# Both orders of a query block in one attention step

## The chip, the cores and the metric

The kernel runs on one core of one Trainium2 chip. The metric is device time in microseconds of one execution, as the median of several. A difference of about 0.2% (some 4.3 us) is the least that a measurement of this kernel can tell from none.

## The reference

Two layers of a hybrid decoder over 512 tokens of width 1024, all in 32-bit floats. Each layer projects x to queries, keys and values of a windowed attention, to those of a retention, and to gates; merges the two branches; then runs a SwiGLU feed-forward. Both sublayers end in a residual and a layer norm. What the change touches is the attention:

```python
for gi, (window, dilation) in enumerate(ATTN_GROUPS):      # (128,1), (512,4), (2048,16)
    o, lse = _dilated_window_attention(q_a[:, :, gi], k_a[:, :, gi], v_a[:, :, gi], ...)
...
s = jnp.einsum('bghnqe,bghnke->bghnqk', qs, kb).astype(jnp.float32) * (Dh ** -0.5)
s = s + bias[None, None, :, None]
m = jnp.max(s, axis=-1, keepdims=True)
p = jnp.exp(s - m)
l = jnp.sum(p, axis=-1, keepdims=True)
o = jnp.einsum('bghnqk,bghnke->bghnqe', (p / l).astype(v.dtype), vb)
...
wts = jax.nn.softmax(jnp.stack(lses, axis=0), axis=0)
y_a = jnp.sum(wts[..., None] * jnp.stack(outs, axis=0), axis=0)
```

There are three groups of six heads, each head 64 wide. A query attends to keys at distances that are multiples of its group's dilation, within the window. The three groups' outputs are mixed with weights that follow from their softmax denominators.

## The kernel before

TensorE (PE) runs nearly all the time on projections. A 32-bit operand is split into a high part (`whi`, `xh`; cast on ACT, line 353 or 94) and a low part (`wlo`, `xl`; subtracted on DVE, line 359 or 95), and a product is three matmuls, high by high, high by low and low by high (`mm3`). Most projections are done as seven products of halves instead of eight (`wide`, `tall`), whose operands are sums of blocks (`xs`; sums of `raw` tiles on DVE, line 375, or in the DMA). Their sums are in PSUM tiles named `ps`, and ACT and DVE copy them out and combine them (`sn`). Weight parts are in rings of four tiles each, raw weights in a ring of eight.

The attention runs beside the projections. Six heads are taken as three pairs (`hp`), and `attention_pair` makes for each pair a list of small operations. A list `side` holds them; each time a projection has emitted three matmuls, `tick` adds to a credit, and for each whole credit the next operation of the list is emitted. `pace(us)` sets the rate so that the list lasts about so long; an operation `nothing` only takes a place. `drain()` emits what is left. The framework's scheduler may then set an engine's instructions in another order than that of emission. Each engine runs its own in order.

A block is 128 queries of both heads of the pair, in one of two orders (`od`): in order 0 the tokens are in their own order, for the group of dilation 1, with 256 keys (128 for the first block); in order 1 they are gathered by their place modulo 4, and hold the groups of dilations 4 and 16, with 128 keys each. Four query blocks (`i`, NI = 4) by two orders are eight blocks a pair. A block goes through three steps:

- `scores(i, od)`: matmuls of 64 contraction rows (one head's width), one head on the upper and one on the lower half of the array, into two PSUM tiles `px` (one a head). DVE adds the bias and takes the maximum (line 571), ACT takes the exponential and its sum (line 573), into a tile `s` of a ring of six (`wk`, tag `w2`), which also holds `sn` and others.
- `turn(i, od)`: PE transposes the exponentials by 128 x 128 (line 582) into the first `px`, and ACT copies them to a tile `sT` of the same ring (line 583).
- `values(i, od)`: matmuls whose result is 64 partitions of a head, both heads side by side, into the second `px`; ACT copies them to `y` (line 595).

For the first two pairs the order at each place is `scores` of block t, `values` of block t-2, `turn` of block t-1; for the last pair it is `turn` of t-1, `scores` of t, `values` of t-1. After the last block `swap` sends maxima and sums of order 1 through DRAM, and a `tail` of operations, inserted into the next pair's list, weighs and adds the groups' outputs.

Of the kernel before, what the change touches and what calls it, by code (L numbers as in the profile page):

```python
# [11 lines left out]
F32 = mybir.dt.float32  # L12
F32R = mybir.dt.float32r
I32 = mybir.dt.int32
AF = mybir.ActivationFunctionType
ALU = mybir.AluOpType
# [3 lines left out]
P = 128  # L20
# [3 lines left out]
NI = S // P  # L24
DEPTH = 2
HD = 64
# [28 lines left out]
def hybrid_kernel(ctx, tc, x, rel_bias, w_in, b_in, w_attn_proj, w_ret_proj, w_out,  # L55
# [491 lines left out]
    def attention_pair(hp, qk, v, yp, bias, yaT):  # L547
# [7 lines left out]
        def scores(i, od):  # L555
            tk = slice(i * P, (i + 1) * P)
            pxs = [psum() for _ in range(2)]
            j0 = 1 if od == 0 and i == 0 else 0
            prs = [slice(hh * HD, (hh + 1) * HD) for hh in range(2)]
            if od == 0:  # L560
                for px, pr in zip(pxs, prs):
                    mm(px[:, j0 * P:2 * P], qk[0][pr, 0, tk], qk[0][pr, 1, (i - 1 + j0) * P:(i + 1) * P], True, True)
            else:
                for j in range(2):
                    for px, pr in zip(pxs, prs):
                        mm(px[:, j * P:(j + 1) * P], qk[1 + j][pr, 0, tk], qk[1 + j][pr, 1, tk], True, True)
            s = wk.tile([P, 2, 2 * P], F32, tag="w2", name="s")
            n0 = j0 * P
            for hh in range(2):
                m_, l_ = nm[:, od, i, hh:hh + 1], ls[:, od, i, hh:hh + 1]  # L570
                dve.tensor_tensor_reduce(out=s[:, hh, n0:], in0=pxs[hh][:, n0:2 * P], in1=bias[hp][hh][:, od, n0:],
                                         scale=-1.0, scalar=3e38, op0=ALU.add, op1=ALU.min, accum_out=m_)
                act.activation(out=s[:, hh, n0:], in_=s[:, hh, n0:], func=AF.Exp, bias=m_, scale=-1.0, accum_out=l_)
            wrk[i, od] = (pxs, s, j0)

        def turn(i, od):
            pxs, s, j0 = wrk[i, od]
            sT = wk.tile([P, 2, 2 * P], F32, tag="w2", name="sT")
            px = pxs[0].rearrange("p (h c) -> p h c", h=2)
            for hh in range(2):  # L580
                for j in range(j0, 2):
                    pe.transpose(px[:, hh, j * P:(j + 1) * P], s[:, hh, j * P:(j + 1) * P], ident)  # L582
            act.copy(out=sT[:, :, j0 * P:], in_=px[:, :, j0 * P:])
            latest["sT"] = sT
            wrk[i, od] = (pxs, sT, j0)

        def values(i, od):
            pxs, sT, j0 = wrk.pop((i, od))
            px = pxs[1]
            vs = (v[i - 1][:, 0] if i else None, v[i][:, 0]) if od == 0 else (v[i][:, 1], v[i][:, 2])  # L590
            for j in range(j0, 2):
                for hh in range(2):
                    cs = slice(hh * HD, (hh + 1) * HD)
                    mm(px[cs, :P], vs[j][:, cs], sT[:, hh, j * P:(j + 1) * P], j == j0, j == 1)
            act.copy(out=y[:, od, i], in_=px[:, :P])
# [61 lines left out]
        blocks = [(i, od) for i in range(NI) for od in range(2)]  # L657
        ops = []
        order = ((0, scores), (2, values), (1, turn)) if hp < 2 else ((1, turn), (0, scores), (1, values))
        for t in range(len(blocks) + 2):  # L660
            for lag, f in order:
                if 0 <= t - lag < len(blocks):
                    ops.append(lambda f=f, b=blocks[t - lag]: f(*b))
                elif t >= len(blocks):
                    ops.append(nothing)
            if t == 0:
                ops += [nothing] * 2
# [712 lines left out]
```

## Time and profile before

| what | value |
|---|---|
| median of the runs | 2147.03 us (2146.54 to 2148.25, 3 runs) |
| span of the profiled execution | 2144.4 us, first to last instruction; the page gives no other time of that execution |
| median less that span | 2.6 us |
| PE busy | 2129.8 us, 13914 matmul records |
| DVE busy | 1492.6 us |
| ACT busy | 1066.1 us |
| DMA | 351.32 MB, mean 164 GB/s |

In a profile's rows, PE is the matmul, PEld its weight load, DVE, ACT and POOL the other engines. A row names line, engine, operation, out<-in by the program's tile names, and shapes; for PE the first pair of numbers is the part of the array that is used (rows*columns). Matmuls overlap: a record's duration is longer than the step to the next one's start, so density is read from starts. A matmul of full 32-bit operands on half the array shows as two records.

### The profile page before, as it was taken

Reading aid. Unit: us, or ns where it says so; the run is one execution under the profiler, and the core shown is the slowest. Engines: PE = TensorE matmul, PEld = TensorE weight load, DVE = VectorE, ACT = ScalarE, POOL = GpSimd, SP = SyncE. Lnnn points to the kernel's source line nnn. Section 1 sums busy time; section 2 is a strip of 40 time slices with the busy share of each in tenths; the row PEclk is TensorE's granted clock in tenths of the full one; section 3 lists DMA queues with packets and bytes.
Section 4 is the critical chain, followed back from the end, with each engine's and each line's share of the span. In section 5 each row is a group of like instructions: output and inputs, shape, how many; then the busy total and the mean of one; then the engine's idle time right before and its main releaser. Section 6 shows DMA issues by size and latency. Waiting matters only on the chain.

```text
span 2144.4 us, 34733 instructions
## 1 busy us (share of the span) xinstructions
PE 2129.8 (99%) x13914; PEld 1917.5 (89%) x13914; DVE 1492.6 (70%) x2113; ACT 1066.1 (50%) x1665; POOL 237.0 (11%) x249
## 2 busy tenths in 40 slices
PE   9999999999999999999999999999999999999998
PEld 8988888889988899989899888888899889999996
DVE  7666898787744776747687567887867357666575
ACT  5566655655623353525255665555666234444350
POOL 4111111111000101000120111101010001010001
PEclk9999999999999999999999999999999999999999
DMA  8865457677776266656258554768687662666561
GB/s 244 216 158 135 125 146 192 168 183 177 232 265 198 60 167 148 165 130 163 75 159 219 145 127 119 182 148 207 161 202 249 227 189 57 187 140 172 114 165 40
DMA packets 313410, 351.32 MB, mean 164 GB/s; under 512 B 22045, under 2 KB 251585, under 8 KB 313120
## 3 DMA queue, kind: packets, MB, share of 16 engines
q1 hardware_dynamic: 227712, 253.01, 38.7%
q0 software_dynamic: 58256, 83.29, 20.7%
q10 hardware_dynamic: 27280, 12.80, 2.1%
q8 instruction: 109, 1.79, 0.3%
q14 instruction: 53, 0.43, 0.1%
HBM read 323.26 MB, written 28.53 MB: 164 GB/s over the span
## 4 chain that ended last, share of the span: by engine, by line
PE 93%; issue 4%; DVE 2%; ACT 1%; POOL 1%; DMA 0%; POOLq 0%; DVEq 0%; SPq 0%; ACTq 0%
PE ps L83 83%; PE px L83 7%; PE px L582 1%; PE px L1045 1%; PE px L192 0%; POOL ry L134 0%; DMA raw<-in_w_in 0%; DVE wlo L359 0%; DVE xtok L1175 0%; PE px L646 0%; ACT whi L353 0%; DVE raw L375 0%; DVE xtok L1184 0%; ACT xh L94 0%; DVE stats L1186 0%
## 5 line engine op out<-in xcount | busy, mean ns | idle before, releaser
L359 DVE TENSOR_TENSOR wlo<-raw,whi 128x1024 fp32r<-128x1024 f32 (+1 forms) x462 | 538.7, 1169 | 249.0 <-ACT whi L353 239.5
L353 ACT CAST whi<-raw 128x1024 fp32r<-128x1024 f32 (+1 forms) x462 | 461.3, 1002 | 465.7 <-PE ps L83 264.4
L83 PE MATMUL ps<-xs,whi 128*128 128x256 f32 (+1 forms) x2944 | 576.3, 294 | 0.0
L83 PEld LDWEIGHTS ps<-xs,whi 128*128 128x128 f32 x2944 | 467.0, 191 | 19.1 <-issue 6.1
L83 PE MATMUL ps<-xs,wlo 128*128 128x256 f32 (+1 forms) x1472 | 430.1, 292 | 0.6 <-DVE wlo L359 0.6
L83 PE MATMUL ps<-xh,whi 128*128 128x256 f32 (+1 forms) x1424 | 425.3, 300 | 2.0 <-ACT xh L94 1.4
L83 PE MATMUL ps<-xh,wlo 128*128 128x256 f32 (+1 forms) x1424 | 418.5, 295 | 1.0 <-DVE wlo L95 1.0
L83 PE MATMUL ps<-xl,whi 128*128 128x256 f32 (+1 forms) x1424 | 419.5, 295 | 0.0
L83 PEld LDWEIGHTS ps<-xh,whi 128*128 128x128 f32 x1424 | 270.8, 191 | 18.6 <-issue 5.1
L83 PEld LDWEIGHTS ps<-xs,wlo 128*128 128x128 f32 x1472 | 281.5, 191 | 6.0 <-DVE wlo L359 1.1
L83 PEld LDWEIGHTS ps<-xl,whi 128*128 128x128 f32 x1424 | 272.2, 191 | 8.0 <-DVE xl L95 0.6
L83 PEld LDWEIGHTS ps<-xh,wlo 128*128 128x128 f32 x1424 | 271.8, 191 | 7.5 <-DVE wlo L95 1.2
L95 DVE TENSOR_TENSOR wlo<-raw,whi 128x1024 fp32r<-128x1024 f32 (+2 forms) x108 | 125.4, 1163 | 156.4 <-ACT whi L94 156.0
L83 PE MATMUL ps<-whi,xs 128*128 128x512 f32 (+1 forms) x768 | 225.0, 362 | 0.2 <-ACT sn L498 0.2
L94 ACT CAST whi<-raw 128x1024 fp32r<-128x1024 f32 (+2 forms) x108 | 107.8, 1001 | 213.8 <-PE ps L83 137.7
L83 PE MATMUL ps<-whi,ht 128*128 128x512 f32 x576 | 178.4, 389 | 0.0
L344 POOL DMA_DIRECT2D raw<-in_w_in x80 | 98.8, 1266 | 681.7 <-DMA raw<-in_w_in 259.3
L375 DVE TENSOR_TENSOR raw<-raw 128x1024 f32<-128x1024 f32 (+1 forms) x132 | 153.9, 1166 | 7.9 <-DMA raw<-in_w_in 5.5
L83 PEld LDWEIGHTS ps<-whi,xs 128*128 128x128 f32 x768 | 137.8, 188 | 19.7 <-ACT sn L498 0.4
L83 PE MATMUL ps<-wlo,xs 128*128 128x512 f32 (+1 forms) x384 | 138.3, 360 | 0.1
L83 PEld LDWEIGHTS ps<-whi,ht 128*128 128x128 f32 x576 | 108.2, 188 | 22.4
L344 POOL DMA_DIRECT2D raw<-in_w_ffn_gate x40 | 51.8, 1294 | 680.1 <-DMA raw<-in_w_ffn_up 289.6
(207 smaller groups left out, 2912.7 us busy)
## 6 DMA issues: line engine op xcount, KB each, us to landing
raw<-in_w_in SPq DMA_DIRECT2D x168, 512.0 KB, 5.1
raw<-in_w_in POOLq DMA_DIRECT2D x64, 512.0 KB, 8.3
raw<-in_w_ffn_up SPq DMA_DIRECT2D x64, 512.0 KB, 4.3
raw<-in_w_ffn_gate SPq DMA_DIRECT2D x44, 512.0 KB, 4.6
raw<-in_w_ffn_down SPq DMA_DIRECT2D x44, 512.0 KB, 3.8
raw<-in_w_ffn_gate POOLq DMA_DIRECT2D x40, 512.0 KB, 6.7
raw<-in_w_ret_proj SPq DMA_DIRECT2D x32, 512.0 KB, 6.3
raw<-in_w_in SPq DMA_DIRECT2D x56, 256.0 KB, 5.0
```

Source lines behind the costliest of these rows:

```text
L83: pe.matmul(ps, lhsT=a, rhs=b, start=start, stop=stop, skip_group_check=True)
L94: act.copy(out=hi, in_=src)
L95: dve.tensor_tensor(out=lo, in0=src, in1=hi.bitcast(F32), op=ALU.subtract)
L344: pool.dma_start(r, self.src({"P1": "B12", "P3": "B22"}[n], u), accum_op=ALU.add)
L353: act.copy(out=h, in_=src)
L359: dve.tensor_tensor(out=l, in0=src, in1=h.bitcast(F32), op=ALU.subtract)
L375: dve.tensor_tensor(out=r, in0=r, in1=self.t["B22" if n == "P2" else "B21", u], op=ALU.add)
L582: pe.transpose(px[:, hh, j * P:(j + 1) * P], s[:, hh, j * P:(j + 1) * P], ident)
L1045: pe.transpose(px[:, t * P:(t + 1) * P], ys[i][:, t * P:(t + 1) * P], ident)
```

## The change

The three steps take a query block with both orders at once. `scores(i)` makes the scores of both orders, order 0 in columns 0 to 255 and order 1 in columns 256 to 511 of each head's PSUM tile, and then the four adds and four exponentials, into two tiles `s`, one an order. `turn(i)` transposes order 0 in the first PSUM tile and order 1 in the second; the copies write the transposed blocks back into the tiles `s` that the exponentials came from, and there is no `sT`. `values(i)` puts both orders' results side by side in the first PSUM tile, and one copy writes both to `y`. The list of a pair is written by a table: `scores` of blocks 0 to 3 at places 0, 7, 14 and 20, `turn` 6 places and `values` 9 places after its `scores`, for all three pairs alike. The list has 32 entries with `swap`, where it had 30 for the first two pairs and 31 for the last.

```diff
-        def scores(i, od):
+        def scores(i):
             tk = slice(i * P, (i + 1) * P)
             pxs = [psum() for _ in range(2)]
-            j0 = 1 if od == 0 and i == 0 else 0
+            j0 = 1 if i == 0 else 0
             prs = [slice(hh * HD, (hh + 1) * HD) for hh in range(2)]
-            if od == 0:
+            for px, pr in zip(pxs, prs):
+                mm(px[:, j0 * P:2 * P], qk[0][pr, 0, tk], qk[0][pr, 1, (i - 1 + j0) * P:(i + 1) * P], True, True)
+            for j in range(2):
                 for px, pr in zip(pxs, prs):
-                    mm(px[:, j0 * P:2 * P], qk[0][pr, 0, tk], qk[0][pr, 1, (i - 1 + j0) * P:(i + 1) * P], True, True)
-            else:
-                for j in range(2):
-                    for px, pr in zip(pxs, prs):
-                        mm(px[:, j * P:(j + 1) * P], qk[1 + j][pr, 0, tk], qk[1 + j][pr, 1, tk], True, True)
-            s = wk.tile([P, 2, 2 * P], F32, tag="w2", name="s")
-            n0 = j0 * P
+                    mm(px[:, (2 + j) * P:(3 + j) * P], qk[1 + j][pr, 0, tk], qk[1 + j][pr, 1, tk], True, True)
+            ss = [wk.tile([P, 2, 2 * P], F32, tag="w2", name="s") for _ in range(2)]
             for hh in range(2):
...
+                for od in range(2):
+                    n0 = j0 * P if od == 0 else 0
+                    s = ss[od]
+                    m_, l_ = nm[:, od, i, hh:hh + 1], ls[:, od, i, hh:hh + 1]
+                    dve.tensor_tensor_reduce(out=s[:, hh, n0:], in0=pxs[hh][:, od * 2 * P + n0:(od + 1) * 2 * P],
+                                             in1=bias[hp][hh][:, od, n0:], scale=-1.0, scalar=3e38,
+                                             op0=ALU.add, op1=ALU.min, accum_out=m_)
+                    act.activation(out=s[:, hh, n0:], in_=s[:, hh, n0:], func=AF.Exp, bias=m_, scale=-1.0, accum_out=l_)
+            wrk[i] = (pxs, ss, j0)
+
+        def turn(i):
+            pxs, ss, j0 = wrk[i]
+            for od in range(2):
+                j1 = j0 if od == 0 else 0
+                px = pxs[od].rearrange("p (h c) -> p h c", h=2)
                 for hh in range(2):
...
+                    for j in range(j1, 2):
+                        pe.transpose(px[:, hh, j * P:(j + 1) * P], ss[od][:, hh, j * P:(j + 1) * P], ident)
+                act.copy(out=ss[od][:, :, j1 * P:], in_=px[:, :, j1 * P:])
+            latest["sT"] = ss[1]
+
+        def values(i):
+            pxs, sTs, j0 = wrk.pop(i)
+            px = pxs[0]
+            for od in range(2):
+                j1 = j0 if od == 0 else 0
+                vs = (v[i - 1][:, 0] if i else None, v[i][:, 0]) if od == 0 else (v[i][:, 1], v[i][:, 2])
+                for j in range(j1, 2):
+                    for hh in range(2):
+                        cs = slice(hh * HD, (hh + 1) * HD)
+                        mm(px[cs, od * P:(od + 1) * P], vs[j][:, cs], sTs[od][:, hh, j * P:(j + 1) * P], j == j1, j == 1)
+            act.copy(out=y[:, :, i], in_=px[:, :2 * P].rearrange("p (o t) -> p o t", o=2))
...
-        order = ((0, scores), (2, values), (1, turn)) if hp < 2 else ((1, turn), (0, scores), (1, values))
...
+        places = [[] for _ in range(30)]
+        for i in range(NI):
+            for at, f in ((0, scores), (6, turn), (9, values)):
+                places[(0, 7, 14, 20)[i] + at].append(lambda f=f, i=i: f(i))
+        ops = [f for p_ in places for f in p_ or [nothing]]
         ops.append(swap)
```

More of the change, by code (lines that the diff above doesn't have):

```diff
@@ L561, in scores @@
                 for px, pr in zip(pxs, prs):
-                    mm(px[:, j0 * P:2 * P], qk[0][pr, 0, tk], qk[0][pr, 1, (i - 1 + j0) * P:(i + 1) * P], True, True)
-            else:
-                for j in range(2):
-                    for px, pr in zip(pxs, prs):
-                        mm(px[:, j * P:(j + 1) * P], qk[1 + j][pr, 0, tk], qk[1 + j][pr, 1, tk], True, True)
-            s = wk.tile([P, 2, 2 * P], F32, tag="w2", name="s")
-            n0 = j0 * P
-            for hh in range(2):
[L570 to L591, printed above, removed]
-                for hh in range(2):
-                    cs = slice(hh * HD, (hh + 1) * HD)
-                    mm(px[cs, :P], vs[j][:, cs], sT[:, hh, j * P:(j + 1) * P], j == j0, j == 1)
-            act.copy(out=y[:, od, i], in_=px[:, :P])
+                    mm(px[:, (2 + j) * P:(3 + j) * P], qk[1 + j][pr, 0, tk], qk[1 + j][pr, 1, tk], True, True)
@@ L655, in combine @@
                 dve.tensor_tensor(out=yr, in0=yr, in1=y[:, od], op=ALU.add)
-        blocks = [(i, od) for i in range(NI) for od in range(2)]
-        ops = []
-        order = ((0, scores), (2, values), (1, turn)) if hp < 2 else ((1, turn), (0, scores), (1, values))
[L660 to L667, printed above, removed]
+        places = [[] for _ in range(30)]
[3 more added lines that the diff above has]
+        ops = [f for p_ in places for f in p_ or [nothing]]
         ops.append(swap)
```

## The prediction

> **What bounds the kernel now.** I read the page's shares first, then its chain, then one stretch of the list of instructions in order of time on PE, and last the busy times by stretch.
>
> ```profile
> PE 2129.8 (99%) x13914; PEld 1917.5 (89%) x13914; DVE 1492.6 (70%) x2113; ACT 1066.1 (50%) x1665; POOL 237.0 (11%) x249
> PE 93%; issue 4%; DVE 2%; ACT 1%; POOL 1%; DMA 0%; POOLq 0%; DVEq 0%; SPq 0%; ACTq 0%
> 107.00:233.00 126.00, 125.71 (x989) 104.30 (x988) 81.75 (x184) 85.48 (x216) 13.12 (x16) 1.00 0.53 131
> ```
>
> PE is idle for 14.6 us of 2144.4 (2144.4 - 2129.8), and the chain that ended last is PE for 93%. The third row is the stretch in which the first layer's three head pairs run: columns are stretch, length, then busy time and instructions of PE, PEld, DVE, ACT and POOL, granted clock, DMA share, GB/s. There PE stands still for 0.3 us in 126, DVE is busy 81.75/126 = 65%, ACT 85.48/126 = 68%, and the clock is full. So what counts is how much time PE's own instructions take from one start to the next, and the attention's work on the other engines costs only what PE waits for it. "Busy" does not settle how dense PE is, so I look at starts.
>
> ```profile
> 110.59 0.28 PE L83 MATMUL ps<-xh,wlo 128*128 128x256 f32 x1
> 110.80 0.71 PE L83 MATMUL px<-qk 64*128 64x128 f32 x8
> 111.45 0.50 PE L83 MATMUL ps<-xs,whi 128*128 128x256 f32 x2
> 111.79 0.28 PE L83 MATMUL ps<-xs,wlo 128*128 128x256 f32 x1
> 111.91 0.40 PE L83 MATMUL ps<-xs,whi 128*128 128x256 f32 x2
> 112.15 0.28 PE L83 MATMUL ps<-xs,wlo 128*128 128x256 f32 x1
> 112.27 0.38 PE L582 MATMUL px<-ident,s 128*128 128x128 f32 x2
> 112.40 0.48 PE L83 MATMUL ps<-xs,whi 128*128 128x256 f32 x2
> 112.72 0.28 PE L83 MATMUL ps<-xs,wlo 128*128 128x256 f32 x1
> 112.84 0.40 PE L83 MATMUL ps<-xs,whi 128*128 128x256 f32 x2
> 113.08 0.28 PE L83 MATMUL ps<-xs,wlo 128*128 128x256 f32 x1
> 113.29 0.70 PE L83 MATMUL px<-qk 64*128 64x256 f32 x4
> 113.92 0.50 PE L83 MATMUL ps<-xs,whi 128*128 128x256 f32 x2
> 114.26 0.28 PE L83 MATMUL ps<-xs,wlo 128*128 128x256 f32 x1
> ```
>
> The first column is the start, the last the number of records that the row merges (a score or value matmul leaves two records, a transpose one). The projection's matmuls (ps) follow each other at 0.12 us: 111.79 to 111.91 is one, 111.91 to 112.15 two. Everything above that pace between two ps rows is the price of the attention burst that stands between them.
>
> **The price of a burst.** Eight score records of 128 columns: 110.59 to 111.79 is 1.20 us and holds three ps matmuls (0.36), so the burst costs 0.84. Four score records of 256 columns: 113.08 to 114.26 is 1.18, less 0.36, is 0.82. Two transposes: 112.15 to 112.72 is 0.57, less 0.36, is 0.21. The same for half as many score records, and for values (px<-sT,v) of four and eight records and four transposes:
>
> ```profile
> 107.48 0.28 PE L83 MATMUL ps<-xh,wlo 128*128 128x256 f32 x1
> 107.69 0.49 PE L83 MATMUL px<-qk 64*128 64x128 f32 x4
> 108.11 0.39 PE L83 MATMUL ps<-xh,whi 128*128 128x256 f32 x1
> 108.33 0.28 PE L83 MATMUL ps<-xl,whi 128*128 128x256 f32 x1
> ...
> 119.18 0.28 PE L83 MATMUL ps<-xs,wlo 128*128 128x256 f32 x1
> 119.39 0.66 PE L83 MATMUL px<-sT,v 128*64 128x128 f32 x8
> 119.98 0.50 PE L83 MATMUL ps<-xs,whi 128*128 128x256 f32 x2
> 120.32 0.28 PE L83 MATMUL ps<-xs,wlo 128*128 128x256 f32 x1
> 120.43 0.40 PE L83 MATMUL ps<-xs,whi 128*128 128x256 f32 x2
> 120.67 0.28 PE L83 MATMUL ps<-xs,wlo 128*128 128x256 f32 x1
> 120.79 0.60 PE L582 MATMUL px<-ident,s 128*128 128x128 f32 x4
> 121.15 0.48 PE L83 MATMUL ps<-xs,whi 128*128 128x256 f32 x2
> 121.47 0.28 PE L83 MATMUL ps<-xs,wlo 128*128 128x256 f32 x1
> ...
> 155.11 0.28 PE L83 MATMUL ps<-xh,wlo 128*128 128x256 f32 x1
> 155.32 0.44 PE L83 MATMUL px<-sT,v 128*64 128x128 f32 x4
> 155.69 0.39 PE L83 MATMUL ps<-xh,whi 128*128 128x256 f32 x1
> 155.91 0.28 PE L83 MATMUL ps<-xl,whi 128*128 128x256 f32 x1
> ```
>
> Four score records: 107.48 to 108.33, 0.85 less two ps (0.24), is 0.61. Four more records therefore cost 0.84 - 0.61 = 0.23, and what is left for no record at all is 0.61 - 0.23 = 0.38 us. Values: eight cost 119.18 to 120.32, 1.14 - 0.36 = 0.78; four cost 155.11 to 155.91, 0.80 - 0.24 = 0.56; so 0.22 for four, and 0.34 for none. Transposes: two 0.21, four 120.67 to 121.47, 0.80 - 0.36 = 0.44: twice as many, twice the price, nothing fixed. The forms say where the fixed part sits: ps and transposes use the array as 128*128, scores as 64*128, values as 128*64. A burst in another shape pays once for going over and coming back: the step from the last ps to the burst is 0.21 instead of 0.12, and the first ps after it takes 0.22 instead of 0.12 (108.11 to 108.33).
>
> [...]
>
> **The change part by part.** *Bursts.* Before, a head pair has eight blocks (four query blocks, two orders), each with a burst of scores, one of transposes and one of values. Now it has four, each with all of both orders. This is the first pair of the first layer on PE; px<-qk are scores, L582 or L584 the transposes, px<-sT,v or px<-s,v the values, ps the projection that runs on beside them. Before, from the second scores to the second transposes:
>
> ```order
> L83 MATMUL px<-qk 128x128 x4
> ...
> L582 MATMUL px<-ident,s 128x128 x2
> ...
> L83 MATMUL px<-qk 128x256 x2
> ...
> L83 MATMUL px<-sT,v 64x128 x2
> ...
> L582 MATMUL px<-ident,s 128x128 x4
> ```
>
> and with the change, from the first scores to the second transposes:
>
> ```order
> L83 MATMUL px<-qk 128x128 x6
> ...
> L584 MATMUL px<-ident,s 128x128 x6
> ...
> L83 MATMUL px<-qk 128x256 x2
> L83 MATMUL px<-qk 128x128 x4
> ...
> L83 MATMUL px<-s,v 64x128 x6
> ...
> L584 MATMUL px<-ident,s 128x128 x8
> ```
>
> Scores of both widths now stand next to each other with no ps between, and so do the values of two blocks. The order counts matmuls; a score or value matmul is two records of the trace. No matmul is added or removed. Three pairs in two layers are 6 x 8 = 48 score bursts and 48 value bursts before. In the order of before the scheduler interleaves scores with transposes twice a layer, which makes 52 score bursts; with the change it splits twice a layer, once after the two 256-wide scores of the first pair's last block, once after the first value matmul of the second pair's last block, which makes 24 + 2 = 26 of each. Saved: 26 x 0.38 = 9.9 us of scores, 22 x 0.34 = 7.5 us of values, nothing for transposes. Sum 17.4 us.
>
> *Transposed blocks go back into s.* The sT tiles go, so a block takes two buffers of the ring of six, held from scores to values, where it took one s and one sT per order. The copy out of PSUM writes what the transposes have read, and waits for nothing that it did not wait for. Price nothing on PE.
>
> *The y copies.* Eight of 128 columns a pair become four of 256; that is ACT work, which is 32% idle there. Nothing on PE.
>
> *The chain between the bursts.* This is the term that the trace of before does not show. DVE and ACT are in order, and now do four adds and four exponentials in a row before the transposes, and two copies before the values. On ACT, first layer, from the first pair's second exponentials on, before:
>
> ```order
> L573 ACTIVATE s,ls<-s,nm 128x256 x2
> L811 ACTIVATE qk<-sn,bQ 128x256
> L811 ACTIVATE qk<-sn,bQ 128x4x64
> L583 COPY sT<-px 128x2x128
> L595 COPY y<-px 128x128
> L573 ACTIVATE s,ls<-s,nm 128x256 x2
> L583 COPY sT<-px 128x512
> ```
>
> and with the change:
>
> ```order
> L585 COPY s<-px 128x2x128
> L585 COPY s<-px 128x512
> L353 CAST whi<-raw 128x1024
> L574 ACTIVATE s,ls<-s,nm 128x256 x4
> L814 COPY sn<-ps 128x512
> L598 COPY y<-px 128x2x128
> ```
>
> Exponentials come in fours, with a weight cast (whi) ahead of them. Their prices:
>
> ```profile
> 111.79 0.41 DVE L571 CUSTOM_DVE_ANT_0 s<-px,bias 128x256 f32<-128x256 f32 x1
> 112.59 0.51 ACT L573 ACTIVATE s<-s,nm 128x256 f32<-128x256 f32 x1
> 113.10 0.49 ACT L573 ACTIVATE s<-s,nm 128x256 f32<-128x256 f32 x1
> L353 ACT CAST whi<-raw 128x1024 fp32r<-128x1024 f32 x406 | 423.8, 1048 | 434.5 <-PE ps L83 246.8 <-issue 104.6 <-DVE raw L375 54.1
> ```
>
> One add (0.4), then four exponentials at the step of 0.51 (112.59 to 113.10), is 2.5 us; with some 0.4 for hand-overs, 2.9 from the scores' end to the transposes, and 3.9 with one cast of 1.05 before it. PE's rows of the change put 36 ps matmuls between the first block's scores and transposes, 4.3 us at 0.12, and 12 + 24 of them and a value burst of six matmuls (twelve records, 0.34 + 0.66 = 1.0) for the second: 5.3 us. So the chain fits with one cast and misses by 0.7 with two (5.0 against 4.3). From below the term can be a small gain, since waits of before can go too: all PE idling in that stretch is 0.3 us a layer, so at most about 1 us. From above: 24 blocks each 0.7 late is 17 us. I take nothing, nearer to the lower end, because the rows put one cast, not two, ahead of most groups of four and ACT has a third of its time free to catch up; for the range I let 8 us of it in.
>
> *Cover.* The 17.4 us leave PE, so everything that was hidden behind it must be ready sooner: 2.9 us a pair of about 42 (126/3). DVE at 65% and ACT at 68% become 70% and 73%. That is no bound.
>
> **The sum.** Against the profiled span of 2144.4: 2127.0. The median of the runs shown, 2147.03, lies 2.6 above that span; with it, 2129.6. I say 2129.5, 0.8% less.
>
> **The rivals.** *Late chain, eaten gain.* PE waits at the transposes or values of about half the blocks for 0.7 us: 12 x 0.7 = 8 us back, 2138. For it: both copies now stand ahead of the values, and near a pair's end only 9 ps matmuls lie between transposes and values. Against: most gaps are above 3.9 us.
>
> *The fixed price belongs to the kind of matmul.* If a 128-wide score after a 256-wide one pays as if it came from the projection, merged scores save nothing, and values alone give 7.5: 2139.5. No row of before shows the two side by side; the form 64*128 is the same for both, which speaks against it.
>
> *Hidden anyway.* A later stage waits for weights that come no sooner, and the gain is lost there: 2146. For it: the DMA engines are busy for 0.53 of the stretch already. Against: PE's 93% of the chain, DMA's 0%.
>
> *Slower: ACT's queue of fours.* If the exponentials of every block stand behind three casts (3.15 us), the chain is 2.9 + 3.15 = 6.05 against 4.3, and PE, in order, waits 1.75 us at each of 24 transposes with the projection queued behind: 42 us, less 17.4, is 2172. It decides from 17.4/24 = 0.73 us a block on. Against: the rows show it nowhere for all blocks.
>
> **Chances.** My forecast 0.72; late chain 0.11; kind of matmul 0.07; hidden 0.06; slower 0.04. Faster by over 0.2% (4.3 us, about what a measurement of this kernel can tell from none) holds the first three: 0.90; within 0.2%, 0.06; slower, 0.04. Range: the lower end takes the 1 us of old waits and 2 us for rounding of the fixed prices (0.01 to 0.04 on 48 bursts), 2126.5; the upper end lets in the late chain and stops at 2138.5, short of the kind of matmul.
>
> **What will show it.** Merged scores of 4 and 8 records should cost 0.44 + 0.46 + 0.38 = 1.28 us above the pace where the two cost 1.66 apart, and 16 value records 0.44 + 0.44 + 0.34 = 1.22 where two bursts cost 1.56. The two kinds should have no ps between them, transposes should still cost 0.11 each, and the same stretch should be some 8.7 us shorter in each layer. I am wrong in size if the fixed part comes twice in a merged burst, and in mechanism if PE's idle time before px<-ident,s or px<-s,v, or the weights' waits on PE, grow by several us.

## The result and the profile after

| | before | changed kernel |
|---|---|---|
| median of the runs | 2147.03 us | 2133.2 us (2132.97 to 2134.82, 5 runs) |
| ratio | 1 | 0.9937, 95% interval 0.9925 to 0.9949 |
| span of the profiled execution | 2144.4 us | 2131.3 us |

The gain is 13.8 us by the medians and 13.1 by the spans; 17.5 and 17.4 were forecast. The time lies within the range, 3.7 us above the forecast. The lines that answer to the first three of before are the page's shares, its chain and the first layer's attention stretch:

```profile
PE 2113.2 (99%) x13914; PEld 1917.3 (90%) x13914; DVE 1488.1 (70%) x2113; ACT 1060.9 (50%) x1641; POOL 239.5 (11%) x249
PE 89%; issue 4%; DVE 3%; ACT 2%; DMA 1%; POOL 1%; POOLq 0%; DVEq 0%; ACTq 0%
107.00:233.00 126.00, 125.10 (x1033) 111.01 (x1032) 87.16 (x192) 87.04 (x209) 14.05 (x17) 1.00 0.53 134
```

PE got 44 more records into the same 126 us (1033 against 989), but it now stands still for 0.9 us there, not 0.3, and the chain has lost four points of PE to DVE, ACT and DMA. So the work became cheaper, and something began to wait. PE's instructions in order of time show the cheaper part. Columns are start, duration, engine, line, operation, tiles, shapes, merged records:

```profile
115.99 0.28 PE L83 MATMUL ps<-xs,wlo 128*128 128x256 f32 x1
116.20 1.15 PE L83 MATMUL px<-qk 64*128 64x256 f32 x12
117.28 0.50 PE L83 MATMUL ps<-xs,whi 128*128 128x256 f32 x2
117.62 0.28 PE L83 MATMUL ps<-xs,wlo 128*128 128x256 f32 x1
...
126.85 0.28 PE L83 MATMUL ps<-xs,wlo 128*128 128x256 f32 x1
127.06 1.09 PE L83 MATMUL px<-s,v 128*64 128x128 f32 x16
128.08 0.51 PE L83 MATMUL ps<-xs,whi 128*128 128x256 f32 x2
128.43 0.28 PE L83 MATMUL ps<-xs,wlo 128*128 128x256 f32 x1
```

A merged score burst costs 117.62 - 115.99 - 0.36 = 1.27 us above the projection's pace (1.28 forecast), and sixteen value records 1.58 - 0.36 = 1.22 (1.22); eight transposes, by the same subtraction, 0.87 (0.88). Summed in this way over every burst of the execution (with 0.23 us a step where the projection's matmuls are 512 columns wide), the attention on PE cost 98.1 us before, in 138 bursts, and 82.8 after, in 74.

The new wait is in the list of what PE waited for, in which no transposes (line 584 now, 582 before) stood before. Columns are the waiting engine, tile and line, the releaser, total us, times, longest:

```profile
PE px L584 <- DVE nm L571: 1.5, 2, 1.1
PE px L584 <- ACT s L574: 1.1, 2, 0.6
```

Both pairs of waits are at one place: the first block of the second head pair, once a layer. The burst of six transposes costs 0.66 us elsewhere; there 2.16 in the first layer and 2.91 in the second. Here is the first of them, the three engines and ACT's DMA issues (ACTq) in order of time, with rows between them left out. The bracket at a row's end is the engine's idle time before it, and what ended it:

```profile
145.26 0.41 ACTq L615 DMA_DIRECT2D mb<-exd  x1
145.71 0.37 ACT L598 COPY y<-px 128x256 f32<-128x256 f32 x1 [3.20 <-DMA exd<-pk]
147.62 0.17 DVE L621 TENSOR_TENSOR mn<-nm,mb 128x8 f32<-128x8 f32 x1 [2.91 <-DMA mb<-exd]
147.83 0.94 PE L83 MATMUL px<-qk 64*128 64x128 f32 x12
149.15 0.16 DVE L631 TENSOR_TENSOR fa<-ea,wa 128x8 f32<-128x8 f32 x1
149.27 0.37 ACTq L630 DMA_DIRECT2D exd<-wb  x1
149.68 1.05 ACT L353 CAST whi<-raw 128x1024 fp32r<-128x1024 f32 x1 [1.36 <-DVE fa L631]
150.76 1.23 DVE L359 TENSOR_TENSOR wlo<-raw,whi 128x1024 fp32r<-128x1024 f32 x1 [1.45 <-ACT whi L353]
151.91 0.28 DVE L571 CUSTOM_DVE_ANT_0 s<-px,bias 128x128 f32<-128x128 f32 x1
152.78 0.33 PE L584 MATMUL px<-ident,s 128*128 128x128 f32 x1 [0.35 <-DVE nm L571]
```

The scores run on PE from 147.83, and by their row's length of 0.94 us their adds could begin about a microsecond later. But DVE's order of instructions holds two things ahead of the adds: the weighing of the first pair's groups (lines 621 to 631), which waits for the trip of maxima and sums through DRAM; then the split of a weight tile (wlo), which waits for ACT's cast, and that stands behind the issue of the weighing's own transfer. In the kernel before, the adds stood between the weighing and that split, and it was DVE that waited for PE:

```profile
148.56 0.16 DVE L628 TENSOR_TENSOR fa<-ea,wa 128x8 f32<-128x8 f32 x1
149.51 0.29 DVE L571 CUSTOM_DVE_ANT_0 s<-px,bias 128x128 f32<-128x128 f32 x1 [0.80 <-PE px L83]
...
150.16 1.22 DVE L359 TENSOR_TENSOR wlo<-raw,whi 128x1024 fp32r<-128x1024 f32 x1
```

The trip itself also took longer. From the issue of its first transfer to the weighing it was 8.1 us (139.51 to 147.62) where the kernel before took 6.0 (141.08 to 147.04), so the weighing came no sooner although PE was ahead.

The other part of the shortfall lies at 92 us, before any attention: a weight tile of the last projection before it landed 1.8 us later (DVE could use it at 91.65 us, not 89.88). The stretch up to 105 us has 8.3 us of PE waits, not 6.7, where every step above the pace by more than 0.15 us is counted. The two programs hold the same instructions in the same order on ACT, DVE and POOL up to there, and on SP up to the value loads of 89 us.

### The profile page after: what moved, and what is told of

The parts are those of the page before. It is cut to its first block, busy times and chain, and to the rows that moved or that the text cites. A ratio compares the mean times of both kernels' runs of the same rounds, so it can differ in the third digit from the quotient of the medians.

```text
span 2131.3 us, 34718 instructions
## 1 busy us (share of the span) xinstructions
PE 2113.2 (99%) x13914; PEld 1917.3 (90%) x13914; DVE 1488.1 (70%) x2113; ACT 1060.9 (50%) x1641; POOL 239.5 (11%) x249
## 4 chain that ended last, share of the span: by engine, by line
PE 89%; issue 4%; DVE 3%; ACT 2%; DMA 1%; POOL 1%; POOLq 0%; DVEq 0%; ACTq 0%
PE ps L83 81%; PE px L83 6%; DVE wlo L359 1%; PE px L584 1%; PE px L1042 1%; ACT whi L353 1%; ACT s L574 1%; DMA exd<-pk 1%; PE px L192 1%; POOL ry L134 0%; DVE xtok L1172 0%; DMA raw<-in_w_in 0%; DVE raw L375 0%; PE px L649 0%; DMA mb<-exd 0%
```

## The experiments

My theory: the price per burst is right, and what is missing was lost at the second pair's first transposes, because the adds stand behind the weighing, and that behind the exchange through DRAM. Rivals: the wait comes from the weight split alone; from the place of the transposes in PE's order; from the ring of buffers; or it is an accident of one execution. Ten other kernels ran, and the changed kernel twice more. "PE's attention" is the sum over bursts as above; the waits are the prices of the six transposes in the first and second layer, 0.66 being a burst without a wait.

| kernel | median us | ratio, 95% interval | span | PE's attention | the two transposes |
|---|---|---|---|---|---|
| changed kernel | 2133.2 | 0.9937, 0.9925 to 0.9949 | 2131.3 | 82.8 | 2.16, 2.91 |
| again | 2135.3 | 0.9936, 0.9924 to 0.9949 | 2134.4 | 84.6 | 2.68, 3.24 |
| a third time | 2134.7 | 0.9941, 0.9929 to 0.9952 | 2132.9 | 84.1 | 1.88, 3.60 |
| exchange issued sooner | 2134.0 | 0.9934, 0.9922 to 0.9947 | 2133.9 | 84.3 | 2.25, 3.34 |
| scores apart | 2146.4 | 1.0000, 0.9990 to 1.0011 | 2142.7 | 89.5 | 1.70, 1.70 |
| values apart | 2136.2 | 0.9949, 0.9935 to 0.9962 | 2133.3 | 86.5 | 1.37, 1.39 |
| no exchange | 2129.8 | 0.9922, 0.9908 to 0.9935 | 2130.3 | 79.9 | 0.66, 0.66 |
| exchange held | 2144.6 | 0.9996, 0.9987 to 1.0004 | 2142.5 | 84.0 | 0.66, 0.66 |
| values and scores joined | 2130.4 | 0.9920, 0.9906 to 0.9933 | 2130.3 | 77.9 | 0.66, 0.66 |
| two blocks a step | 2139.3 | 0.9962, 0.9950 to 0.9975 | 2135.1 | 73.8 | none of six |
| own tiles for the transposed | 2136.4 | 0.9946, 0.9933 to 0.9959 | 2130.7 | 82.9 | 2.18, 3.11 |
| transposes later | 2141.1 | 0.9971, 0.9961 to 0.9981 | 2145.5 | 90.3 | 3.30, 2.06 |
| joined, weights later | 2130.9 | 0.9925, 0.9913 to 0.9937 | 2132.6 | 79.3 | 0.66, 0.66 |

### The price of a burst: one half undone at a time

The scores in two operations, one side step apart:

```diff
-            for at, f in ((0, scores), (6, turn), (9, values)):
+            for at, f in ((0, scores), (1, scores1), (6, turn), (9, values)):
...
```

> The change, but the scores of order 0 one place before those of order 1, with projection matmuls between; adds, exponentials, transposes, values and the table of places as in the change. Theory (each burst in another array shape pays 0.38 us for scores): 48 score bursts in place of 26, 22 x 0.38 = 8.4, less 2 value bursts that the scheduler no longer splits (0.7): 7.7 us more, 2141. Rival (the gain comes from fewer and wider instructions on DVE and ACT, or from the places): below 2135.

The values in two operations, an order each:

```diff
-            for at, f in ((0, scores), (6, turn), (9, values)):
+            for at, f in ((0, scores), (6, turn), (9, lambda i: values(i, 0)), (10, lambda i: values(i, 1))):
...
```

> The change, but the values of order 0 one place before those of order 1, with projection matmuls between; one y copy for both as in the change. Theory (0.34 us a value burst): 46 value bursts in place of 26, 20 x 0.34 = 6.8, less 2 score bursts that are no longer split (0.8): 6.0 us more, 2139. Rival (as for the scores): below 2135.

Scores apart, PE in order of time:

```profile
116.35 0.28 PE L83 MATMUL ps<-xs,wlo 128*128 128x256 f32 x1
116.56 0.70 PE L83 MATMUL px<-qk 64*128 64x256 f32 x4
117.19 0.51 PE L83 MATMUL ps<-xs,whi 128*128 128x256 f32 x2
117.53 0.29 PE L83 MATMUL ps<-xs,wlo 128*128 128x256 f32 x1
...
117.89 0.28 PE L83 MATMUL ps<-xs,wlo 128*128 128x256 f32 x1
118.10 0.72 PE L83 MATMUL px<-qk 64*128 64x128 f32 x8
118.75 0.50 PE L83 MATMUL ps<-xs,whi 128*128 128x256 f32 x2
119.08 0.28 PE L83 MATMUL ps<-xs,wlo 128*128 128x256 f32 x1
```

The same twelve records cost 0.82 + 0.83 = 1.65 us in two bursts and 1.27 in one: 0.38 for the second burst. Over the execution the score bursts cost 8.7 us more, where 22 x 0.38 is 8.4. PE's attention as a whole grew by 6.7 us, because value bursts that are no longer split saved 1.1 and the waits at the two transposes fell by 1.7, against 0.8 more at other transposes. So the rival that a 128-wide score pays even behind a 256-wide one is out. The median is 2146.4 us where 2141 was expected, and the span rose by 11 us, more than the bursts account for: PE's waits at projection and weights' matmuls grew by 4.4 us as well, above all before the transposes of the weights (1.4 and 1.5 us), where POOL's expanding copy came late.

Values apart, the value bursts cost 35.5 us where they cost 29.0 together: 6.5 for 20 more bursts, 0.33 each, as priced. The span rose by 2.0 only, and the median is 2136.2 us where 2139 was expected: the waits at the two transposes fell by 2.3 us, PE's waits at projection matmuls by 1.1, and two score bursts that the scheduler no longer cut in two saved 0.8. Both prices stand; the sum of time does not follow them alone, because each edit also moves the exchange against the next pair's scores.

### What the wait at the second pair's transposes comes from

The exchange's first step put six side steps earlier in the list:

```diff
+        places[24].append(swap)
         ops = [f for p_ in places for f in p_ or [nothing]]
-        ops.append(swap)
+        ops.append(nothing)
```

> The change, with swap (the sending of order 1's maxima and sums) at place 24, right after the last scores, in place of the list's end. PE's order is the same. Theory: the second pair's first exponentials are late because DVE and ACT, in order, stand before them waiting for the first pair's numbers to come back through DRAM; sent some 2 us sooner, they come back sooner, the 3.7 us of waits at L584 shrink to below 1.5, and the time is 2130 to 2132. Rival: the wait comes from the weight cast and subtraction that stand ahead of the adds on ACT and DVE, whatever the exchange does; then nothing moves, 2133.

A miss. Nothing moved: the first transfer was issued at 139.49 us (139.51 before the edit), the second at 145.07 (145.26), because each engine's order is set by a scheduler, which had put the first step there already. This is no test of the theory.

The trip left out:

```diff
-            act.dma_start(exd.rearrange("(l r) c -> l r c", r=4), pk)
...
-            act.dma_start(mb, exd.rearrange("(i p) c -> p i c", p=P))
...
-            dve.tensor_tensor(out=mn, in0=nm[:, 0], in1=mb[:, :, 0:2], op=ALU.min)
+            dve.tensor_tensor(out=mn, in0=nm[:, 0], in1=nm[:, 1], op=ALU.min)
```

> Edit to the changed kernel: the weights of a head pair (weigh) read the second order's maxima and sums directly, without the trip through DRAM that regroups them by token; pk, exd and mb and their two transfers per pair are gone. It leaves out this regrouping, so the weights that it computes belong to other tokens; all else, and PE's work, stays. Theory: TensorE waits at the first transposes of the second head pair (2.16 us in layer 0 and 2.91 us in layer 1 where 0.66 is the price without a wait) because VectorE stands in its queue behind the weigh step, and that behind the transfer of mb; with the transfer gone both waits fall below 1.0 us, and the span comes 3 to 4.5 us below that of the changed kernel (2131.3): 2127 to 2128.5, a median of 2129 to 2130.5. Rival: the wait comes from the split of a projection tile (whi on ScalarE, wlo on VectorE, 2.3 us together) that lies ahead of the adds anyway: then the waits stay above 1.5 us each, and the time within 1.5 us of 2133.

```profile
147.92 0.94 PE L83 MATMUL px<-qk 64*128 64x128 f32 x12
...
148.88 1.23 DVE L359 TENSOR_TENSOR wlo<-raw,whi 128x1024 fp32r<-128x1024 f32 x1 [4.07 <-PE px L83]
150.02 0.28 DVE L571 CUSTOM_DVE_ANT_0 s<-px,bias 128x128 f32<-128x128 f32 x1
...
152.36 0.82 PE L584 MATMUL px<-ident,s 128*128 128x128 f32 x6
```

Six transposes in one piece, with no wait, in both layers. The weight split still stands directly ahead of the adds, but it starts 1.9 us sooner (148.88, not 150.76). So the wait needs the exchange, and the split alone does not make it. The exchange alone does not make it either, as far as the kernel before shows: its weighing ended about as late, but its adds stood ahead of the split, and no transposes waited. No run moves the split behind the adds in the changed kernel. The margin is small even here: the block's last exponential ends at 152.12 us, 0.2 us before the transposes.

The median, 2129.8, is 3.4 us below the changed kernel's first and lies in the range that was expected. In the profiled execution the span is only 1.0 lower: PE waited 1.83 us more at one transposing of the weights in the first layer, and the bursts behind it ran slower, at a granted clock of 0.50 from 211.5 to 212.5 us (see the last section).

The exchange kept, but its second transfer held behind the next pair's first exponentials:

```diff
+            latest["s"] = ss[1]
...
+            act.copy(out=mb, in_=latest["s"][:, 1, :4 * NI].rearrange("p (i c) -> p i c", i=NI))
             act.dma_start(mb, exd.rearrange("(i p) c -> p i c", p=P))
```

> Edit to the changed kernel: a 16-element copy into mb from the exponentials of the next head pair's first block stands ahead of the transfer of mb, so that this transfer, and the weigh step that waits for it, start only behind that block's adds and exponentials. Nothing is left out. Theory: the two waits at the second pair's first transposes fall below 1.0 us (from 2.16 and 2.91), as without the exchange, and the span comes 2.5 to 4 us below 2131.3; the weigh step then falls among the adds of the second block, whose transposes come 7 us behind its scores, so that no new wait over 0.5 us appears. Rival: the wait only moves, to the second block's transposes or to the transposes of the weights (the four records px<-ident,fe), by 1.5 us or more each, and the time stays within 1.5 us of 2133.

Both waits went, as the theory says, but later steps then came late, and PE waited longer there, as the rival says. The time, 2144.6 us, is above what either gave. For the weights' transposes of the third pair:

```profile
208.61 0.28 PE L83 MATMUL ps<-xs,wlo 128*128 128x256 f32 x1
211.93 0.94 PE L651 MATMUL px<-ident,fe 128*128 128x128 f32 x4 [3.04 <-POOL fe L645]
```

The same in the second layer, beside 2.4 us in each layer at other transposes: a span of 11 us more in all. The split stands directly ahead of the first block's adds here too, with no wait behind it.

The transposes put later, so that 27 projection matmuls stand ahead of them and not 18:

```diff
-        places = [[] for _ in range(30)]
+        places = [[] for _ in range(32)]
...
-                places[(0, 7, 14, 20)[i] + at].append(lambda f=f, i=i: f(i))
+                places[(0, 9, 16, 22)[i] + at + (2 if i == 0 and at else 0)].append(lambda f=f, i=i: f(i))
```

> Edit to the changed kernel: in each pair's list the transposes of the first block stand two places later and all that follows one to two places later, so that 27 projection matmuls (6.3 us) stand between the second pair's first scores and their transposes, not 18 (4.2 us). Nothing is left out. Theory: TensorE's waits at these transposes (2.16 and 2.91 us) are lateness of 1.5 and 2.25 us of the adds against a fixed place; 9 matmuls are 2.1 us, so the first wait goes to 0.66 and the second to 0.66 to 0.8, and the span falls by 3.5 to 4 us if nothing else moves into a wait, 2127.5; with one new wait of the weights' transposes, as two earlier runs had it, 2129 to 2131. Rival: the lateness follows the transposes (the adds wait for a resource that the transposes free): waits stay over 1.5 us, 2133.

A miss: 2141.1 us, where 2131 was the most that the theory gave. The profiled execution, with a span of 2145.5 us, lies above the kernel's median. DVE and PE at the second pair of the first layer:

```profile
145.69 0.94 PE L83 MATMUL px<-qk 64*128 64x128 f32 x12
...
149.15 0.17 DVE L629 TENSOR_TENSOR wb<-ea,wa 128x8 f32<-128x8 f32 x1
...
151.99 0.28 DVE L571 CUSTOM_DVE_ANT_0 s<-px,bias 128x128 f32<-128x128 f32 x1
152.86 0.33 PE L584 MATMUL px<-ident,s 128*128 128x128 f32 x1 [1.50 <-DVE nm L571]
```

The adds did not move (151.91 to 151.99), although the scores stood 2.1 us sooner (147.83 to 145.69). They stood sooner because in this execution all did: the first scores of the layer are at 107.22 us, not 109.46. The exchange's second transfer was issued 2.1 us sooner as well (143.18, not 145.26), but it landed 4.4 us after that and not 2.3, so the weighing was no sooner. From the weighing's wb to the first add it is 151.99 - 149.15 = 2.84 us, and the same 2.84 in the changed kernel (149.07 to 151.91; in the second layer 1205.69 to 1208.53). So the adds hang on the exchange, as the theory has it. The nine more matmuls bought about 2.1 us, and the slower transfer took 2.1: this run does not show that a later place is worth nothing by itself. In the second layer, where the transfer took 2.8 us, the transposes' price fell from 2.91 to 2.06. The longer list brought new waits of 2 to 3 us at the weights' transposes, and a median 6.4 us above that of the changed kernel beside it.

### The second part of the change

```diff
-                act.copy(out=ss[od][:, :, j1 * P:], in_=px[:, :, j1 * P:])
+                sT = wk.tile([P, 2, 2 * P], F32, tag="w2", name="sT")
+                act.copy(out=sT[:, :, j1 * P:], in_=px[:, :, j1 * P:])
...
```

> Edit to the changed kernel: its second part is undone. The transposed blocks go into tiles of their own (sT, from the same ring of eight as the exponentials), not back into the exponentials' tiles. Nothing is left out; TensorE's order is that of the changed kernel. Theory: the in-place copy saves ring slots only, no engine works more or less, so the time is that of the changed kernel within 1.5 us (2131.7 to 2134.7), if the ring's eight tiles still cover a block; attention's cost on TensorE stays 82 to 84 us. Rival (the ring was what mattered): an exponentials' tile now comes free later, adds wait for it, waits at transposes come to 5 us or more in all: 2138 or more.

(The ring has six tiles, not eight as written there.) PE's attention is 82.9 us against 82.8, the span 2130.7 against 2131.3, the two transposes 2.18 and 3.11. The median, 2136.4, is above the expected 2134.7 and 1.7 above the changed kernel's beside it, with runs from 2132.2 to 2139.5 and intervals that overlap; it does not reach the rival's 2138. The copy back into the exponentials' tiles does nothing that the trace shows.

The changed kernel itself, twice more:

> The changed kernel once more, for what repeats. Theory: the changed kernel falls short of the forecast by two things, PE waiting at the first transposes of the second head pair (1.5 us in the first layer, 2.2 us in the second, above the 0.66 us that six transposes cost), which is made by the kernel and comes again, and weights that landed 1.7 us late at 91 us of the profile, before any attention, which is chance. So 2132 to 2134 us, with the wait at L584 again and the late weights somewhere between nothing and 1.8 us. Rival: the late weights belong to the change (SyncE's order of loads moved) and come again in full.

> The changed kernel as it is, for a comparison on the same chip with the three runs beside it. Theory: 2132 to 2136 us, waits at the second pair's first transposes between 2.1 and 3.3 us each, as in its two earlier profiles. Rival (the waits are an accident of one execution): one of the two below 1 us.

The transposes with a wait are there in all three profiles, at prices between 1.88 and 3.60 us; they are no accident, though their size varies more than expected. The medians are 2135.3 us, above the 2132 to 2134 that was expected, and 2134.7, as expected. The start's 8.3 us came back too (8.1 and 8.5). But kernels with the same order up to there have 6.7 (transposes later), 6.8 (two blocks a step) and 7.3 (exchange held), so it is scatter in when weights land, or something in the programs that I did not find; what it is stays open.

### Fewer changes of shape

Values of block i-1 and scores of block i as one operation:

```diff
+        def join(i):
+            if i:
+                values(i - 1)
+            if i < NI:
+                scores(i)
...
+        places = [[] for _ in range(37)]
+        for i in range(NI + 1):
+            places[9 * i].append(lambda i=i: join(i))
+            if i < NI:
+                places[9 * i + 6].append(lambda i=i: turn(i))
+        places[31].append(swap)
```

> Edit to the changed kernel: the values of block i-1 and the scores of block i are one operation, so that 18 of the 24 value bursts stand directly ahead of a score burst with no projection matmul between (82 runs of attention matmuls in TensorE's order become 67, weights' transposes counted). Nothing is left out. If the price of 0.38 and 0.34 us is one for leaving the 128x128 shape and coming back, a value burst with a score burst behind it pays it once: 18 times 0.34 to 0.38, 6.1 to 6.8 us less. If each change of shape costs its own half (three changes in place of four), 18 times 0.18, 3.2 us less. Rival: the price belongs to the two kinds of burst, not to the change: nothing. Against each stand waits from the longer list (the two waits at the second pair's first transposes stay, 2 to 5 us in all; the same 0 to 2 us of start). The time: 2126.5 to 2127.5, 2130, or 2133.

```profile
126.35 0.28 PE L83 MATMUL ps<-xs,wlo 128*128 128x256 f32 x1
126.56 1.09 PE L83 MATMUL px<-s,v 128*64 128x128 f32 x16
127.59 1.15 PE L83 MATMUL px<-qk 64*128 64x256 f32 x12
128.66 0.50 PE L83 MATMUL ps<-xs,whi 128*128 128x256 f32 x2
129.00 0.28 PE L83 MATMUL ps<-xs,wlo 128*128 128x256 f32 x1
```

2.65 less three ps (0.36) is 2.29 us, where the two bursts cost 1.22 + 1.27 = 2.49: 0.20 saved, at 16 of the 18 joints (12 of this size, 4 with twelve value records at 2.08 against 2.27; the other two hold waits). So neither outer case holds, but the middle one: three changes of shape in place of four. If going over and coming back cost alike, one change is by estimate 0.17 to 0.19 us (half of 0.34 and of 0.38), and going straight from values to scores some 0.16 (0.34 + 0.38 - 0.20, less 0.17 and 0.19).

One rival is left. Scores and values differ from the projection not only by the shape: their operands are full 32-bit numbers, where the projection's are the parts of a split in another type (fp32r), and no run changes the one without the other. For the shape speak the transposes, which are full 32-bit at 128*128 and pay nothing fixed (0.21 us for two, 0.44 for four), and this joint, where both neighbours are full 32-bit and a change still costs some 0.16. The price of a burst, and that merging saves it, do not depend on which it is.

Of the kernels that leave nothing out, the joined one is the fastest by the median, 2130.4; its interval overlaps that of the changed kernel. The waits that were expected at the second pair's transposes did not come; it has others, before the weights' transposes among them (1.45 and 1.37 us). Here the exchange was quick: issues at 140.63 and 143.07 us, the weighing at 144.98.

Two query blocks a step:

```diff
...
+        for g in range(2):
+            for at, f in ((0, scores), (8, turn), (13, values)):
+                places[15 * g + at].append(lambda f=f, g=g: f(g))
+        places[21].append(swap)
```

> Edit to the changed kernel: one step takes two query blocks, so that the 24 score bursts, 24 value bursts and 24 transpose bursts become 12 each of twice the length. Nothing is left out. By the prices of the prediction 12 times 0.38 and 12 times 0.34 us go, 8.6 us: 2124.6 if no new wait comes. The chain between scores and transposes is twice as long (8 adds of 0.55 us with exponentials behind), and the table leaves 24 to 51 projection matmuls between them (5.6 to 12 us). The first case (the price alone): 2123.5 to 2126. The second case (new waits for the longer chain eat more than half): 2129 to 2135, with waits over 1.5 us at transposes or values in at least four places.

(In the changed kernel an add of 256 columns took 0.42 us, with 0.35 from one start to the next, not 0.55 as written there.)

The price held: 24 score records cost 2.15 us where two bursts cost 2.54, and 32 value records 2.08 where two cost 2.44, and PE's attention fell by 9.0 us. For the time, new waits ate more than all of it, as in the second case, but the median, 2139.3 us, lies above that case's range too, and the waits stand elsewhere: 1.4 us a layer at a projection matmul between the transposes, and 4.9 and 4.3 us after the attention, at a projection that waits for ACT's copies (line 498).

The joined kernel with the weights' transposes later:

```diff
-                for at, f in zip((30, 29, 27, 19, 17, 15, 13, 12, 3), reversed(tail)):
+                for at, f in zip((33, 32, 29, 23, 21, 19, 13, 12, 3), reversed(tail)):
```

> The kernel with values of block i-1 and scores of block i in one operation (2130.4 us), with the weights' transposes three to four places later in each list, because TensorE waited 1.61 and 1.5 us there for GpSimd's expanding copy, which stood behind an accumulating DMA. Nothing is left out. Theory: these two waits go, 3 us: 2127.4, and 2126.5 to 2128.5 with noise. Rival: the copy gets later with its reader, since the DMA ahead of it in GpSimd's queue waits for TensorE: 2130.4 within 1.5 us.

The two waits went, and others of 1.49 and 2.67 us came at the last pair's weights' transposes: no gain, 2130.9 us, as the rival says. That the copy came later for the reason that the rival gives is not shown.

## Why the prediction was right, and where it was short

*The bound.* Right: PE, 99% busy before and after, sets the time, and what counts is its steps from start to start.

*The price of a burst, and the bursts.* Right, within 0.01 us a burst; that the price is one of the shape is likely, not shown. Without the waits at three transposes (1.50, 2.25, and 0.20 in the second layer's first pair) PE's attention would be 98.1 to 78.8, 19.3 us less; 17.4 were forecast. Some 1.2 us of the difference lie in bursts of before that the scheduler had cut up with transposes, which cost more than I counted: four transposes and two times two score records of 256 columns 2.09 us, where my prices give 0.44 + 0.46 + 2 x 0.38 = 1.66. Most of the rest are three bursts of before that had a gap of 0.15 us beside them and cost 0.22 more than priced.

*The second part, the y copies, the cover.* Right: nothing to be seen.

*The chain between the bursts.* This is the step that failed: "I take nothing". It cost 3.95 us at three transposes. I had worked it out from the length of the adds and exponentials against the matmuls between scores and transposes, with one weight cast ahead, and that held in 21 of 24 blocks. But I took the matmuls from the first pair, 36 between scores and transposes; at the second pair's first block there are 18. And what I left out is that the adds stand there in DVE's order behind the weighing of the pair before, whose data come through DRAM, with the weight split between the two. With one order a step, scores of order 0 alone, the adds went ahead of the weight split; with both orders they come after it. The trace of before had the rows, the order of the change had the new place of the adds, and I had compared ACT's order there, not DVE's. The 0.4 us for hand-overs in the chain's length was an estimate: in the changed kernel an exponential began 0.03 us behind the maximum that it needs (152.20 to 152.23), and a transpose 0.05 behind the exponential that it waited for (153.60 to 153.65).

*The sum.* By spans: 19.3 less 3.95, less 1.5 at the start, less 0.5 elsewhere, is 13.3, and 13.1 were measured. That the time missed by no more than 3.7 us is in part luck: the bursts gave 1.9 more than forecast, which covers a third of the 6 us lost. The late chain was named as a rival at 8 us for half of all blocks; it came at half that, in one block a layer, by another mechanism.

*What would show it.* The merged prices came as written, 1.27 and 1.22. From the last projection matmul before the attention to one and the same matmul behind it, the stretch became 7.9 and 6.0 us shorter in the two layers, where 8.7 were written. The sign that I gave for a wrong mechanism, idle time before px<-ident,s that grows by several us, did appear: none was listed before, 2.6 us after. It belongs to the term of the chain; the price of the bursts, whose own sign would have been a fixed part paid twice, stands.

## What to carry to other kernels

Where TensorE sets the time, as here with 99% of the span, sum what each burst of another array shape costs from start to start: here each such burst had a fixed price, 0.38 us for scores and 0.34 for values, and putting like next to like saved it to within 0.01 us. When work is merged, look at what stands ahead of its first reader in that engine's own order, above all anything that waits for a round trip through DRAM (8.1 us in the changed kernel's first layer); the length of the chain alone does not show it. And a place that is moved later covers a wait only as far as what is waited for stays where it is; where that hangs on a trip whose length varies, as here (2.3 and 4.4 us from issue to landing for one transfer in two kernels), the gain can vanish.

## What was new about the hardware

Some waits of TensorE cost more than their length here: behind them the granted clock was half. The kernel with the exchange held, where this lasted 3.41 us, in stretches of that length (columns as in the prediction: PE's busy time stands behind the comma, the clock is the third number from the end):

```profile
208.76:212.17 3.41, 0.37 (x4) 0.24 (x3) 3.41 (x10) 1.68 (x4) 1.06 (x2) 1.00 0.95 206
212.17:215.58 3.41, 3.41 (x18) 3.19 (x18) 3.41 (x11) 0.62 (x1) 0.00 (x0) 0.50 0.73 79
215.58:219.00 3.42, 3.42 (x34) 3.16 (x33) 1.58 (x4) 1.17 (x2) 0.00 (x0) 1.00 0.53 107
```

The wait of 3.04 us ended at 211.93, and 3.41 us at half speed are an estimated 1.7 us more. The third profile of the changed kernel had it as well, behind waits of 1.56 and 0.55 us at the second layer's transposes; ps steps are 0.21 us there, not 0.12:

```profile
1209.56 0.33 PE L584 MATMUL px<-ident,s 128*128 128x128 f32 x1 [1.56 <-DVE nm L571]
1210.43 1.11 PE L584 MATMUL px<-ident,s 128*128 128x128 f32 x5 [0.55 <-ACT s L574]
...
1211.77 0.41 PE L83 MATMUL ps<-xh,wlo 128*128 128x256 f32 x1
1211.98 0.41 PE L83 MATMUL ps<-xh,whi 128*128 128x256 f32 x1
```

The clock was 0.50 there (1212.0 to 1213.0 us), which is why the scores after those transposes cost 2.22 us in place of 1.27; the 3.60 us of the transposes themselves are mostly the wait. It does not follow each wait: the kernel with later transposes kept its clock behind a wait of 2.16 us, which ended at 210.75, and lost it behind one of 2.29, which ended at 247.03:

```profile
206.07:209.48 3.41, 2.52 (x22) 2.28 (x20) 3.19 (x6) 3.16 (x7) 1.39 (x3) 1.00 1.10 280
209.49:212.90 3.41, 2.15 (x17) 2.01 (x19) 2.15 (x6) 1.26 (x3) 1.21 (x2) 1.00 1.06 256
243.63:247.04 3.41, 1.12 (x6) 0.58 (x5) 2.85 (x3) 0.00 (x0) 2.25 (x2) 1.00 0.35 23
247.04:250.45 3.41, 3.41 (x10) 2.89 (x11) 1.82 (x2) 1.05 (x1) 0.00 (x0) 0.50 0.89 205
```

The rows are cut where the clock changed, at 247.04 and 250.45, and in steps of 3.41 us back from the first of these. Cut so, PE stood idle for 0.9 us of the first row and 1.3 of the second (3.41 less 2.52 and 2.15), with full speed behind each; for 2.3 us of the third (3.41 less 1.12), with half speed behind it, as it was behind 3.0 us in the kernel with the exchange held. What decides it is not shown. The changed kernel's three profiles, with two waits each at the second layer's transposes, lie close together:

| profile | waits, us | granted clock behind them | over, us |
|---|---|---|---|
| changed kernel | 1.10 and 0.55 | 1.00 | 1210.3 to 1213.3 |
| again | 1.17 and 0.55 | 0.73 | 1210.0 to 1213.0 |
| a third time | 1.56 and 0.55 | 0.61 | 1210.4 to 1213.4 |

The length of the wait alone does not decide: the joined kernel with later weights kept a clock of 1.00 (1299.9 to 1302.9 us) behind a wait of 2.67, where the kernel without the exchange lost it behind 1.83 (0.50 from 211.5 to 212.5).

If the price of a burst is one of shape, going from 128*128 to 64*128 and back cost 0.38 us here, going to 128*64 and back 0.34, and both, where values meet scores, 0.20 less than the two together.

The small trip through DRAM was long and uneven. From the issue of its first transfer to that of its second, which waits for the first to land, it took 2.4 us in the joined kernel's first layer, 3.5 in the kernel before, 5.75 in the changed kernel's first layer and 6.5 in its second. How busy the DMA engines were does not explain it: their mean share at the time was, in this order, 0.80, 0.89, 0.94 and 0.75. Why it varies stays open.
